# Ada rows on GpSimd's queue, and in the first stage in three small places of their own

## The chip, the cores and the metric

The kernel runs on one NeuronCore of a Trainium2 chip. The metric is the device time of one execution in microseconds. The engines are called as in the profile: PE (TensorE, with PEld for its weight loads), DVE (VectorE), ACT (ScalarE), POOL (GpSimd) and SP (SyncE). SP and POOL issue transfers; each engine takes its instructions in order.

## What is computed

One transformer layer for 256 tokens of width 2048, in float32. Nine vectors that depend on a condition `c` shift, scale and gate its three parts:

```python
ada = (silu(c) @ w_ada + b_ada)              # [9 * 2048]; w_ada is 2048 x 18432
sh1, sc1, g1, sh2, sc2, g2, sh3, sc3, g3 = split(ada, 9)
h = swiglu(modulate(x, sh1, sc1), ffn1_w_in, ffn1_w_out)          # 2048 -> 2 x 5632 -> 2048
x = layernorm(ALPHA * x + 0.5 * (1 + g1) * h, ln1_g, ln1_b)
h = token_mixer(modulate(x, sh2, sc2), ...)                       # FoX attention and mLSTM heads
x = layernorm(ALPHA * x + (1 + g2) * h, ln2_g, ln2_b)
h = swiglu(modulate(x, sh3, sc3), ffn2_w_in, ffn2_w_out)
x = layernorm(ALPHA * x + 0.5 * (1 + g3) * h, ln3_g, ln3_b)
# modulate(x, sh, sc) = layernorm(x) * (1 + sc) + sh
```

## The kernel before

**Products.** Each weight is brought in as float32 into a large place (tag `raw`, three places of 1 MB) by SP in `load_w` (L371). `split` makes two float32r parts of it: ACT casts the high part (L145) and DVE subtracts it for the low part (L146). The parts lie in six places each, two to a block of 1 MB. `mm3` then takes three matmuls (L388 to L390) for one product.

**Ada rows.** `w_ada` is not multiplied on PE. One row block holds 128 rows by 1024 columns (512 KB); 16 of them make an item. DVE multiplies the first by a column of silu(c) (L158) and adds each further one with a multiply-add (L160) into an accumulator; PE then sums over the partitions by products with ones. `ada_acc` is the helper, and its instructions stay in program order. The small places (tag `araw`, three places of 512 KB) hold such rows; a layernorm's scratch `sq` takes one of them for a while.

**The first stage.** The first matrix of the first feed-forward part is taken in four rounds `j`, each over 512 of the 2048 inputs and twelve blocks of 1 MB in an order given by `order_of(j)`. `first_in` makes the 48 matmuls of a block; the part sums of rounds after the first are added by DVE (L809). A round can begin when its 512 columns of x are modulated, which needs the shift and scale columns, and so 16 ada rows. The rows of round 0 come before all else. Those of round j + 1 are taken during round j by the generator `first_ada`, which is advanced once in most blocks: each call issues two rows and adds them. Two calls of three put the two rows into one large place (L715), the third into two small ones (L709). After the last, PE sums the columns (L736, L752 for round 0), DVE writes `scsh`, and `modulate_both` makes the columns of x. `behind(modulated[0])` queues the adds on DVE behind the last part of the modulation before.

**Later stages.** 14 more items follow, for the gates (`ada_gate`) and the other shifts and scales (`ada_pair`). `pump` is called once per block or so; it first adds the rows that were issued before (`add_landed`) and then issues a few more (`ada_rows`, L168), on SP's queue, into the small places. `need(n)` completes n items where their result is used. The bias of a gate is a transfer on POOL's queue (L208), which waits until the gate's place in `gate` has been read for the last time. POOL also computes the powers for the layernorms (`inv_root`, L268) and the masks of the mixer.

The order of the instructions on each engine and each queue is made ahead of time by a planner from program order and its own costs. DVE's order is written out by hand at the layernorms (`boundary`) and DVE's and ACT's for the end of round 0's rows.

Of the kernel before, what the change touches and what calls it, by code (L numbers as in the profile page):

```python
# [7 lines left out]
F32 = mybir.dt.float32  # L8
F32R = mybir.dt.float32r
AF = mybir.ActivationFunctionType  # L10
ALU = mybir.AluOpType
# [3 lines left out]
P = 128  # L15
T = 256
D = 2048
KD = D // P
# [29 lines left out]
def layer_kernel(  # L48
# [8 lines left out]
    V, S, G_, PE, SP = nc.vector, nc.scalar, nc.gpsimd, nc.tensor, nc.sync  # L57
# [16 lines left out]
    ap = ctx.enter_context(tc.tile_pool(name="ap", bufs=1))  # L74
# [4 lines left out]
    def mm_tile(name):  # L79
        return pm.tile([P, 512], F32, tag="mm", name=name)  # L80

    def aux_tile(name):
        return pa.tile([P, 512], F32, tag="aux", name=name)
# [13 lines left out]
    ones, onesr = triu1[:, P:], trir[:, P:]  # L97
# [8 lines left out]
    cps = aux_tile("cps")  # L106
# [4 lines left out]
    bcol = cst.tile([P, 9, KD], F32, name="bcol")  # L111
# [17 lines left out]
    def load_mixer_smalls():  # L129
        hrow = ap.tile([6, 1024], F32, tag="acc", name="hrow")  # L130
        SP.dma_start(hrow[0:4, :], mlstm_conv_w[0])
        SP.dma_start(hrow[4:5, :], mlstm_conv_b)
        SP.dma_start(hrow[5:6, :], mlstm_norm_g)
        SP.dma_start(gbias[:, 0:8], fox_f_bias[0:1, :].to_broadcast([P, 8]))
        SP.dma_start(gbias[:, 8:12], mlstm_i_bias[0:1, :].to_broadcast([P, 4]))
        SP.dma_start(gbias[:, 12:16], mlstm_f_bias[0:1, :].to_broadcast([P, 4]))
        yield
        hps = aux_tile("hps")
        for i in range(8):
            PE.transpose(hps[:, i * 6:(i + 1) * 6], hrow[:, i * P:(i + 1) * P], ident[:6, :6])  # L140
        V.tensor_copy(hcol.rearrange("p a b -> p (a b)"), hps[:, :48])
# [7 lines left out]
    scsh = cst.tile([P, 9, KD], F32, name="scsh")  # L149
    gate = cst.tile([P, D], F32, name="gate")  # L150


    def pair_cols(v, j):
        return w_ada[0, :, v * D:(v + 2) * D].rearrange("k (v n) -> k v n", v=2)[:, :, j * 512:(j + 1) * 512]

    def ada_acc(acc, raw, k):
        if k == 0:
            ins = V.tensor_scalar_mul(acc, raw, csil[:, k:k + 1])  # L158
        else:
            ins = V.scalar_tensor_tensor(out=acc, in0=raw, scalar=csil[:, k:k + 1], in1=acc,  # L160
                                         op0=ALU.mult, op1=ALU.add)
        tc.keep_in_program_order(ins)


    def ada_rows(acc, src, tag):
        for k in range(KD):
            raw = ap.tile([P, 1024], F32, tag="araw", bufs=3, name=f"ar{tag}_{k}")
            SP.dma_start(raw.rearrange("p (v n) -> p v n", v=2), src[k * P:(k + 1) * P])  # L168
            landing.append((acc, raw, k))
            yield PAUSE if k == KD - 1 else None  # L170

# [121 lines left out]
    def ntag():  # L293
        seq[0] += 1
        return str(seq[0])
# [3 lines left out]
    modulated = [None]  # L299

    def behind(ins):
        return tc.issue_after(ins.ins) if ins else nullcontext()

    def modulate_both(v, j, rs, xT):
        xf = npool.tile([P, 4, T], F32, tag="xf", name=f"xf{ntag()}")
        n = xf.rearrange("p k t -> p (k t)").rearrange("p (a n) -> p a n", a=2)
        for a in range(2):
            S.activation(n[:, a, :], res[:, a, j * 512:(j + 1) * 512], AF.Identity, bias=rs[a][:, 1:2],
                         scale=rs[a][:, 0:1])
        yield  # L310
        tps = [aux_tile(f"tp{ntag()}") for _ in range(2)]
        for q in range(4):
            for a in range(2):
                PE.transpose(tps[q // 2][:, (2 * (q % 2) + a) * P:(2 * (q % 2) + a + 1) * P],
                             n[:, a, q * P:(q + 1) * P], ident)
        yield
        for q in range(4):
            k = 4 * j + q
            S.activation(xf[:, q, :], tps[q // 2][:, (q % 2) * T:(q % 2 + 1) * T], AF.Identity,
                         bias=scsh[:, v, k:k + 1], scale=scsh[:, v + 1, k:k + 1])  # L320
            hi, lo = (x[:, k, :] for x in xT)
            S.copy(hi, xf[:, q, :])
            yield
            modulated[0] = V.tensor_tensor(out=lo, in0=xf[:, q, :], in1=hi.bitcast(F32), op=ALU.subtract)
            yield
# [33 lines left out]
    def new_xT(tag):  # L359
        return (xp.tile([P, KD, T], F32R, name=f"xhi_{tag}"), xp.tile([P, KD, T], F32R, name=f"xlo_{tag}"))  # L360
# [332 lines left out]
    xT = new_xT("f1")  # L693
# [3 lines left out]
    def first_ada(j, ws=iter(())):  # L697
        src = pair_cols(0, j)
        if j % 2:
            acc = ap.tile([P, 2, 512], F32, tag="acc", name=f"acc0_{j}")  # L700
        else:
            acc = gate[:, :1024].rearrange("p (v n) -> p v n", v=2)
        for kk in range(8):
            if kk % 3 == 2:
                raws = []
                for h in range(2):
                    k = 2 * kk + h
                    raw = ap.tile([P, 2, 512], F32, tag="araw", bufs=3, name=f"ar0_{j}_{k}")
                    SP.dma_start(raw, src[k * P:(k + 1) * P])  # L709
                    raws.append(raw)  # L710
            else:
                raw = wp.tile([P, 2, 2, 512], F32, tag="raw", bufs=3, name=f"ar0_{j}_{kk}")
                for h in range(2):
                    k = 2 * kk + h
                    SP.dma_start(raw[:, h], src[k * P:(k + 1) * P])  # L715
                raws = [raw[:, h] for h in range(2)]
            with behind(modulated[0]):
                for h in range(2):
                    k = 2 * kk + h
                    if k < KD - 1:  # L720
                        ada_acc(acc, raws[h], k)
                    else:
                        for b in range(2):
                            bs = slice(b * 256, (b + 1) * 256)
                            ada_acc(acc[:, :, bs], raws[h][:, :, bs], k)
            if kk == 5:
                mb = modulate_both(0, j, rs0, xT)
            if kk in (5, 6):
                next(mb)
            yield  # L730
        cps = aux_tile(f"cp{j}"), mm_tile(f"cq{j}") if j == 0 else None

        def columns():
            for q in range(4):
                for v in range(2):
                    PE.matmul(cps[0][:, 4 * v + q:4 * v + q + 1], acc[:, v, q * P:(q + 1) * P], ones[:, 0:1],  # L736
                              start=True, stop=True)
            js = slice(4 * j, 4 * j + 4)
            V.tensor_tensor(out=scsh[:, 0:2, js], in0=cps[0][:, :8].rearrange("p (v k) -> p v k", v=2),
                            in1=bcol[:, 0:2, js], op=ALU.add)  # L740

        if j:
            columns()
            for _ in mb:
                pass
            yield
            return

        def column(q):
            cp = cps[q % 2][:, q:q + 2]  # L750
            for v in range(2):
                PE.matmul(cp[:, v:v + 1], acc[:, v, q * P:(q + 1) * P], ones[:, 0:1], start=True, stop=True)  # L752
            k = 4 * j + q
            V.tensor_tensor(out=scsh[:, 0:2, k:k + 1], in0=cp.unsqueeze(2), in1=bcol[:, 0:2, k:k + 1], op=ALU.add)

        column(0)
        next(mb)
        column(1)
        next(mb)
        next(mb)  # L760
        column(2)
        next(ws, None)
        next(mb)
        column(3)
        next(mb)
        next(ws, None)
        for _ in mb:
            pass
        yield


    NS = 12

# [60 lines left out]
    fa = first_ada(0, ws_halves())  # L834
    rs0 = [small(2, "mr", f"mr_x{a}") for a in range(2)]
# [16 lines left out]
                   ada_pair(6, 1), ada_gate(5, 0, 1.0), ada_gate(5, 1, 1.0), ada_pair(6, 2), ada_pair(6, 3),  # L852
                   ada_gate(8, 0, 0.5), ada_gate(8, 1, 0.5)]
    for j in range(4):
        fa = first_ada(j + 1) if j < 3 else load_mixer_smalls()
        for n, i in enumerate(order_of(j)):
            w = list(ws if n + j == 0 else first_w(j, i))
            for _ in range(n not in (4, 9, 10)):
                next(fa, 0)
            first_in(j, n, i, w)  # L860
            if j == 3 and n > 2:
                pump(R_F)
# [59 lines left out]
    xT = new_xT("mx")  # L922
    raws = [mo_raw(u) for u in range(3)]
    mow = {}
    fence, _, xs = boundary(*ent["f"], lgb, 3, "1", xT, entry_of(mo_load, mow, 3, 6), KD)
# [337 lines left out]
    for j in (2, 3, 0, 1):  # L1263
        ps = form_a_pair(C_FQ + j * 256, C_FK + j * 256, f"f{j}")
        for i in range(2):
            h = 2 * j + i
# [66 lines left out]
    xT = new_xT("f2")  # L1333
# [31 lines left out]
    for j in range(2, 10):  # L1365
# [3 lines left out]
        if j == 7:  # L1369
            need(11)  # L1370
            mb = modulate_both(6, 2, mr2, xT)
            next(mb)
        ps = half_in(j, 0, "fh")
        for f in range(2):
            i = 2 * j + f
# [11 lines left out]
    mb = []  # L1387
# [7 lines left out]
    for j in range(2, 10):  # L1395
# [7 lines left out]
        for f in range(2):  # L1403
            i = 2 * j + f
# [51 lines left out]
```

## Time and profile before

| | us |
|---|---|
| median of three runs (lowest, highest) | 1946.42 (1943.57, 1947.09) |
| the profiled execution: its time | 1946.44 |
| the profiled execution: span of its instructions | 1944.7 |
| PE busy | 1893.7 |
| DVE busy | 1458.4 |
| ACT busy | 931.4 |
| POOL busy | 19.4 |

The span is the time from the first to the last instruction. The page gives the busy time of each engine, its share of the span, and the number of instructions. Matmuls overlap one another, so PE counts as busy while any is under way; whether it runs at its usual pace is read from the starts of the matmuls. Queries of the trace give the same numbers for stretches of the span (windows), the waits of each engine with what ended them, the instructions in order of time, and the chain of waits that ended last. The columns of a row are told where one is shown. A row of a wait reads: engine, what it was about to do and its line, what it waited for; then the sum in microseconds, how often, and the longest.

### The profile page before, as it was taken

What the parts mean: (1) busy time and instruction counts of PE and PEld (TensorE: products, weight loads), DVE (VectorE), ACT (ScalarE), POOL (GpSimd) and SP (SyncE); (2) the same over time, 40 slices, a digit from 0 to 9 for tenths busy, and PEclk for the clock granted to TensorE, in tenths of its full rate; (3) what the DMA queues carried; (4) which work ended last, traced back from release to release, by engine and by line L of the source; (5) the groups of instructions that cost most, each with busy time, mean ns of one, the idle gap of its engine ahead of it and who ended that gap; (6) DMA issues with size and microseconds to landing.
All of it is one profiled execution on the core that took longest, in us unless ns stands there. A gap on an engine that the chain in (4) does not pass through costs nothing.

```text
span 1944.7 us, 32312 instructions
## 1 busy us (share of the span) xinstructions
PE 1893.7 (97%) x13197; PEld 1737.9 (89%) x13197; DVE 1458.4 (75%) x1753; ACT 931.4 (48%) x1294; POOL 19.4 (1%) x37
## 2 busy tenths in 40 slices
PE   3999999999999999999999999999999999999997
PEld 3999999999988888699999886999999999988886
DVE  7879879777678898678787787677776554555776
ACT  2544354444354454745664644565444444444552
POOL 0000000000000000000000000000000000000000
PEclk9999999999999999999999999999999999999999
DMA  8999969999898798489878884997787755655552
GB/s 324 349 321 318 316 206 313 319 305 332 287 324 306 260 312 270 152 295 305 272 245 281 292 287 148 310 322 266 238 269 253 236 185 192 233 192 195 194 191 90
DMA packets 301963, 510.89 MB, mean 263 GB/s; under 512 B 10834, under 2 KB 158962, under 8 KB 300792
## 3 DMA queue, kind: packets, MB, share of 16 engines
q1 hardware_dynamic: 300952, 505.70, 76.9%
q0 software_dynamic: 864, 3.15, 0.5%
q8 instruction: 103, 1.69, 0.4%
q14 instruction: 44, 0.36, 0.0%
HBM read 506.71 MB, written 2.10 MB: 262 GB/s over the span
## 4 chain that ended last, share of the span: by engine, by line
PE 72%; issue 11%; DVE 9%; DMA 5%; ACT 2%; POOL 0%; SPq 0%; DVEq 0%; ACTq 0%; POOLq 0%
PE gu_f L389 8%; PE gu_f L388 8%; PE gu_f L390 8%; PE o_f L388 8%; PE o_f L390 8%; PE o_f L389 8%; PE s L388 3%; PE s L390 3%; PE s L389 2%; DMA raw_s<-in_ffn_w_in_dram 2%; DMA raw_mxo<-in_w_out_dram 2%; DVE gate L160 2%; PE fh L388 2%; PE fh L389 1%; PE fh L390 1%
## 5 line engine op out<-in xcount | busy, mean ns | idle before, releaser
L160 DVE SCALAR_TENSOR_TENSOR acc<-ar,csil,acc 128x1024 f32<-128x1024 f32 x242 | 307.2, 1270 | 23.2 <-DMA ar<-in_w_ada_dram 22.3
L388 PE MATMUL s<-xhi_f,hi_s 128*128 128x256 f32 x768 | 214.1, 279 | 1.8 <-ACT hi_s L145 1.8
L390 PE MATMUL s<-xhi_f,lo_s 128*128 128x256 f32 x768 | 213.5, 279 | 1.1 <-DVE lo_s L146 1.1
L389 PE MATMUL s<-xlo_f,hi_s 128*128 128x256 f32 x768 | 213.5, 278 | 0.0
L390 PE MATMUL gu_f<-xhi_f,lo_f2i 128*128 128x256 f32 x768 | 212.0, 276 | 0.0
L389 PE MATMUL gu_f<-xlo_f,hi_f2i 128*128 128x256 f32 x768 | 212.0, 276 | 0.0
L388 PE MATMUL gu_f<-xhi_f,hi_f2i 128*128 128x256 f32 x768 | 212.0, 276 | 0.0
L146 DVE TENSOR_TENSOR lo_f2i<-raw_f2i,hi_f2i 128x1024 fp32r<-128x1024 f32 x96 | 117.6, 1225 | 99.8 <-ACT hi_f2i L145 99.7
L388 PE MATMUL gu_f<-xhi_f,hi_f1i 128*128 128x256 f32 x640 | 176.8, 276 | 0.0
L390 PE MATMUL gu_f<-xhi_f,lo_f1i 128*128 128x256 f32 x640 | 176.7, 276 | 0.0
L389 PE MATMUL gu_f<-xlo_f,hi_f1i 128*128 128x256 f32 x640 | 176.7, 276 | 0.0
L145 ACT CAST hi_f2i<-raw_f2i 128x1024 fp32r<-128x1024 f32 x96 | 100.8, 1050 | 137.5 <-PE gu_f L389 125.5
L145 ACT CAST hi_s<-raw_s 128x1024 fp32r<-128x1024 f32 x96 | 97.3, 1048 | 114.4 <-DMA raw_s<-in_ffn_w_in_dram 70.1
L388 PEld LDWEIGHTS s<-xhi_f,hi_s 128*128 128x128 f32 x768 | 145.6, 190 | 2.3 <-ACT hi_s L145 2.3
L390 PEld LDWEIGHTS s<-xhi_f,lo_s 128*128 128x128 f32 x768 | 145.4, 190 | 2.0 <-DVE lo_s L146 2.0
L389 PEld LDWEIGHTS s<-xlo_f,hi_s 128*128 128x128 f32 x768 | 145.7, 190 | 0.0
L389 PEld LDWEIGHTS gu_f<-xlo_f,hi_f2i 128*128 128x128 f32 x768 | 144.2, 188 | 0.1
L388 PEld LDWEIGHTS gu_f<-xhi_f,hi_f2i 128*128 128x128 f32 x768 | 144.2, 188 | 0.1
L390 PEld LDWEIGHTS gu_f<-xhi_f,lo_f2i 128*128 128x128 f32 x768 | 144.2, 188 | 0.0
L146 DVE TENSOR_TENSOR lo_s<-raw_s,hi_s 128x1024 fp32r<-128x1024 f32 x96 | 114.4, 1220 | 38.0 <-ACT hi_s L145 37.7
L145 ACT CAST hh<-hT 128x512 fp32r<-128x512 f32 x128 | 78.6, 621 | 132.7 <-PE o_f L389 132.5
L146 DVE TENSOR_TENSOR lo_f2o<-raw_f2o,hi_f2o 128x1024 fp32r<-128x1024 f32 x88 | 107.7, 1224 | 44.9 <-ACT hi_f2o L145 44.8
(480 smaller groups left out, 5340.7 us busy)
## 6 DMA issues: line engine op xcount, KB each, us to landing
ar<-in_w_ada_dram SPq DMA_DIRECT2D x288, 512.0 KB, 5.9
raw_s<-in_ffn_w_in_dram SPq DMA_DIRECT2D x48, 1024.0 KB, 5.6
raw_f2i<-in_ffn_w_in_dram SPq DMA_DIRECT2D x48, 1024.0 KB, 5.2
raw_f1o<-in_ffn_w_out_dram SPq DMA_DIRECT2D x44, 1024.0 KB, 7.2
raw_f2o<-in_ffn_w_out_dram SPq DMA_DIRECT2D x44, 1024.0 KB, 5.1
raw_f1i<-in_ffn_w_in_dram SPq DMA_DIRECT2D x40, 1024.0 KB, 7.6
raw_mxo<-in_w_out_dram SPq DMA_DIRECT2D x16, 1024.0 KB, 8.6
raw_fh<-in_ffn_w_in_dram SPq DMA_DIRECT2D x16, 1024.0 KB, 7.9
```

Of the source, the lines that this page charges most:

```text
L145: S.copy(hi, src)
L146: V.tensor_tensor(out=lo, in0=src, in1=hi.bitcast(F32), op=ALU.subtract)
L160: ins = V.scalar_tensor_tensor(out=acc, in0=raw, scalar=csil[:, k:k + 1], in1=acc, op0=ALU.mult, op1=ALU.add)
L388: PE.matmul(o, ah, bh, start=start, stop=False)
L389: PE.matmul(o, ah, bl, start=False, stop=False)
L390: return PE.matmul(o, al, bh, start=False, stop=stop)
```

## The change

Ada rows of the later stages are issued from POOL's queue instead of SP's (`ada_rows`). In the first stage, `first_ada` keeps only the rows of round 0, on SP's queue and in large and small places as before. The rows of the other rounds come from a new generator, `next_ada`: it issues two rows per call from POOL's queue, all into the three small places, and adds the two rows of the call before. It has one call more than `first_ada` had, and the loop gives it one more block.

```diff
@@ ada_rows
-            SP.dma_start(raw.rearrange("p (v n) -> p v n", v=2), src[k * P:(k + 1) * P])
+            G_.dma_start(raw.rearrange("p (v n) -> p v n", v=2), src[k * P:(k + 1) * P])
@@ first_ada: its part for j > 0 goes
-        cps = aux_tile(f"cp{j}"), mm_tile(f"cq{j}") if j == 0 else None
-
-        def columns():
-            ...
-        if j:
-            columns()
-            for _ in mb:
-                pass
-            yield
-            return
+        cps = aux_tile(f"cp{j}"), mm_tile(f"cq{j}")
@@ new
+    def next_ada(j):
+        src = pair_cols(0, j)
+        if j % 2:
+            acc = ap.tile([P, 2, 512], F32, tag="acc", name=f"acc0_{j}")
+        else:
+            acc = gate[:, :1024].rearrange("p (v n) -> p v n", v=2)
+        rows = []
+        for k in range(0, KD + 2, 2):
+            with behind(modulated[0]):
+                for raw in rows:
+                    ada_acc(acc, raw, k - 2 + rows.index(raw))
+            rows = []
+            for h in range(2 if k < KD else 0):
+                raw = ap.tile([P, 2, 512], F32, tag="araw", bufs=3, name=f"ar0_{j}_{k + h}")
+                G_.dma_start(raw, src[(k + h) * P:(k + h + 1) * P])
+                rows.append(raw)
+            if k == 10:
+                mb = modulate_both(0, j, rs0, xT)
+            if k in (10, 12):
+                next(mb)
+            yield
+        cp = aux_tile(f"cp{j}")
+        for i in range(8):
+            PE.matmul(cp[:, i:i + 1], acc[:, i // 4, i % 4 * P:(i % 4 + 1) * P], ones[:, 0:1], start=True, stop=True)
+        js = slice(4 * j, 4 * j + 4)
+        V.tensor_tensor(out=scsh[:, 0:2, js], in0=cp[:, :8].rearrange("p (v k) -> p v k", v=2),
+                        in1=bcol[:, 0:2, js], op=ALU.add)
+        for _ in mb:
+            pass
+        yield
@@ the loop over rounds
-        fa = first_ada(j + 1) if j < 3 else load_mixer_smalls()
+        fa = next_ada(j + 1) if j < 3 else load_mixer_smalls()
         for n, i in enumerate(order_of(j)):
             w = list(ws if n + j == 0 else first_w(j, i))
-            for _ in range(n not in (4, 9, 10)):
+            for _ in range(n not in (4, 9)):
                 next(fa, 0)
```

More of the change, by code (lines that the diff above doesn't have):

```diff
@@ L730, in first_ada @@
             yield
-        cps = aux_tile(f"cp{j}"), mm_tile(f"cq{j}") if j == 0 else None
-        def columns():
[L734 to L740, printed above, removed]
-        if j:
-            columns()
-            for _ in mb:
-                pass
-            yield
-            return
+        cps = aux_tile(f"cp{j}"), mm_tile(f"cq{j}")
         def column(q):
```

## The prediction

> **What bounds the kernel now.** I read the page's table of engines first, then the waits of TensorE, then the busy time by windows, then the matmuls in order of time.
>
> ```profile
> span 1944.7 us, 32312 instructions
> ...
> PE 1893.7 (97%) x13197; PEld 1737.9 (89%) x13197; DVE 1458.4 (75%) x1753; ACT 931.4 (48%) x1294; POOL 19.4 (1%) x37
> ...
> PE cp L752 <- DVE gate L160: 14.8, 1, 14.8
> ...
> 200.00:220.00 20.00, 20.00 (x179) 20.00 (x178) 18.49 (x21) 8.00 (x8) 0.00 (x0) 1.00 0.94 322
> 220.00:240.00 20.00, 18.06 (x143) 17.66 (x142) 17.40 (x21) 7.99 (x8) 0.00 (x0) 0.91 0.92 310
> ```
>
> TensorE (PE) is busy for 97% of the span. Its 51 us of idle time lie mostly in the first 38 us, where no weight product can start, and at the three layernorms. A change to transfers can therefore win only what TensorE loses to late data. The windows (columns: stretch, length, then PE, PEld, DVE, ACT and POOL busy with counts, the granted clock, DMA share, GB/s) show one clear loss: 143 matmuls where the window before has 179, with the granted clock at 0.91 instead of 1.00.
>
> ```profile
> 60.07 0.28 PE L389 MATMUL s<-xlo_f,hi_s 128*128 128x256 f32 x1
> ...
> 63.93 0.28 PE L390 MATMUL s<-xhi_f,lo_s 128*128 128x256 f32 x1
> ...
> 227.93 0.28 PE L390 MATMUL s<-xhi_f,lo_s 128*128 128x256 f32 x1
> 229.38 0.38 PE L388 MATMUL s<-xhi_f,hi_s 128*128 128x256 f32 x1 [1.18 <-ACT hi_s L145]
> 230.64 0.58 PE L390 MATMUL s<-xhi_f,lo_s 128*128 128x256 f32 x1 [0.76 <-DVE lo_s L146]
> 231.03 0.41 PE L388 MATMUL s<-xhi_f,hi_s 128*128 128x256 f32 x1
> ...
> 234.01 0.28 PE L390 MATMUL s<-xhi_f,lo_s 128*128 128x256 f32 x1
> ```
>
> From 60.07 to 63.93 there are 34 steps, so a matmul of the first stage takes 3.86 / 34 = 0.1135 us, and a block of 48 takes 5.45 us. From 227.93 to 234.01 there are 18 steps, which should take 2.04 us and take 6.08: **4.04 us are lost**. TensorE waits 1.18 and 0.76 us for split weights, and then runs at a step of 0.21 us until 233.80. The rest of what late data cost shows between the column sums of the blocks of x (16 matmuls each, in order of time):
>
> ```profile
> 102.25 1.84 PE L736 MATMUL cp<-trir,acc 128*128 128x1 f32 x16
> 170.92 1.84 PE L736 MATMUL cp<-trir,gate 128*128 128x1 f32 x16
> 242.97 1.84 PE L736 MATMUL cp<-trir,acc 128*128 128x1 f32 x16
> ```
>
> A round needs 576 x 0.1135 = 65.4 us, 1.7 for the column sums and about 0.8 for eight transposes: 67.9. The first interval is 68.67, the second 72.05. The losses are 0.8 and 4.15, together 4.9 us, of which the hole is 4.04.
>
> Why were the weights late? The chain of waits at that place, then SyncE's own waits and those of the engines from 38 to 245 us (us, times, longest):
>
> ```profile
> 220.62 1.21 DVE acc L160
> 221.85 6.34 DMA raw_s<-in_ffn_w_in_dram
> 228.29 1.05 ACT hi_s L145
> ...
> SPq L371 <- DVE lo_s L146: 68.8, 29, 6.2
> SPq L715 <- DVE lo_s L146: 18.6, 7, 3.5
> SPq L371 <- DVE acc L160: 11.7, 6, 3.7
> ...
> ACT hi_s L145 <- DMA raw_s<-in_ffn_w_in_dram: 70.1, 27, 7.4
> ```
>
> A pair of ada rows held one of the three large `raw` places until its add ended at 221.83; only then could SyncE issue the weights, which took 6.34 us to land. SyncE issues in order, so a row that waits for a place (L715) also holds back the weights behind it.
>
> **The change part by part.** The first edit moves 224 rows (14 items of 16, L168) from SyncE's queue to POOL's, the second 48 of the first stage (three rounds of 16, L709 and L715). Only the 16 rows of the first round stay. The nearest row for a transfer issued by POOL is the bias of the gates, of equal size (512 KB):
>
> ```profile
> L208 POOL DMA_DIRECT2D gate<-in_b_ada_dram x6: 527/599/732, 173.1 to 1196.5; - x6
> DMA to landing us min/median/max: 4.1/5.2/7.3
> ```
>
> 272 issues of 0.6 us are 163 us on POOL, idle 99% of the span: hidden, if nothing urgent stands behind them. SyncE loses as many issues; what they covered was its own queue.
>
> *The large places* then belong to weights. Three blocks (16 us) can be on their way where rows took a share, and the delay from the add at 221.83 to the split goes. I credit the hole, 4.0, and 0.8 of the other 0.9: **-4.8 us**. Bounds: 0 (nothing cured) and -4.9. Late next would be VectorE's own throughput, so here is its load in the three rounds:
>
> ```profile
> 38.50:104.20 65.70, 65.62 (x554) 64.93 (x555) 51.37 (x48) 39.67 (x53) 0.00 (x0) 1.00 0.93 330
> 104.20:174.50 70.30, 69.98 (x616) 69.78 (x616) 60.76 (x68) 30.85 (x38) 0.73 (x1) 1.00 0.94 325
> 174.50:245.30 70.80, 68.86 (x591) 68.46 (x590) 62.73 (x70) 29.22 (x35) 0.00 (x0) 0.98 0.91 312
> ```
>
> VectorE is busy 51.4 + 60.8 + 62.7 = 174.9 of 206.8 us. It can follow TensorE, with 31.9 us to spare. Its work stays the same; the last row of a round is added undivided, which moves it by less than 0.2 us.
>
> *Three small places, two rows per block.* A row's place is free when its add ends; the row three further on must have landed one block later. VectorE's work in such a block is two splits, two adds and, after the first round, two part sums:
>
> ```profile
> L146 DVE TENSOR_TENSOR lo_s<-raw_s,hi_s x75: 1214/1219/1227, 38.5 to 242.8; 128x1024 fp32r<-128x1024 f32 x75
> L160 DVE SCALAR_TENSOR_TENSOR acc<-ar,csil,acc x16: 746/1278/1286, 179.5 to 224.9; 128x1024 f32<-128x1024 f32 x14, 128x512 f32<-128x512 f32 x2
> L809 DVE TENSOR_TENSOR hT<-hT,s x62: 675/680/689, 120.7 to 317.7; 128x512 f32<-128x512 f32 x62
> ```
>
> That is 2 x 1.22 + 2 x 1.28 = 5.0 us in the first round and 5.0 + 2 x 0.68 = 6.4 after it. Issue and landing at the median are 5.2 us (the row of landings above), with up to 0.6 more because a row goes in two pieces per partition. At 5.8 the pairs of the first round wait 0.8 us each, 8 x 0.8 = 6 us inside that round's 14 us of spare time (65.7 - 51.4), and the later ones nothing. I take **0**; the bounds stand with the rivals. "Added a block behind" only shifts the adds; column sums still stand before the twelfth block.
>
> *The start.* The first rows of the second round now leave POOL as soon as a small place is free, beside the last rows and the first weights of the first round:
>
> ```profile
> 20.22 4.87 SPq L715 DMA_DIRECT2D ar<-in_w_ada_dram  x4
> ...
> 26.85 0.37 SPq L371 DMA_DIRECT2D raw_s<-in_ffn_w_in_dram  x1
> ...
> DMA to landing us min/median/max: 3.9/6.8/11.6
> ...
> 33.46 0.77 DVE gate L160
> ...
> 20.00:40.00 20.00, 4.96 (x21) 4.62 (x22) 16.90 (x23) 4.27 (x8) 0.00 (x0) 1.00 0.97 350
> ```
>
> A row is 0.52 MB / 350 GB/s = 1.5 us of the DMA engines. The last row was issued at about 24.7 us (the last of the four), rows up to 50 us land after 6.8 at the median, so at 31.5, and VectorE uses it at 33.46. Two microseconds are to spare: one extra row is covered, a second costs 1.0 at most, and as much may hit the first weights (issued at 26.85). Cost between 0 and 1.5; I take **+0.3**, near the covered end, since the second and third place come free only with the adds of rows ten and eleven.
>
> *The moved queue.* Behind a row on POOL now stand the powers of the layernorms (L268), the memsets of the mixer, and the gate biases (L208); VectorE waits for the powers. At a layernorm:
>
> ```profile
> 768.53 27.07 SPq L168 DMA_DIRECT2D ar<-in_w_ada_dram  x3
> ...
> 796.14 0.55 POOL L268 TENSOR_TENSOR mr<-sums,mhalf 128x1 f32<-128x1 f32 x1 [7.61 <-DVE sums L558]
> 797.65 0.93 PE L340 MATMUL tp<-ident,n 128*128 128x128 f32 x4 [0.54 <-ACT n L336]
> ...
> 676.37 0.53 POOL L208 DMA_DIRECT2D gate<-in_b_ada_dram  x1 [404.70 <-DVE o_f L466]
> ...
> 1012.77 1.65 POOL L268 TENSOR_TENSOR rr<-ss,mhalf 128x8 f32<-128x8 f32 x1 [183.73 <-DVE ss L1202]
> ```
>
> SyncE's third row there waits for the square's scratch (`sq`, a small place), free about when the power at 796.14 runs. If POOL issues that row first, the power comes 0.53 to 0.73 us later, and TensorE, already waiting 0.54 us, with it. Three such places (two layernorms, the mixer at 1012.77) give 0 to 2.2; I take **+0.3**. A gate bias waits for the gate's last reader (404.7 us while POOL had nothing else); it was queued when it became ready, so rows behind it would wait only for the planner's error: 0. SyncE no longer waits at L168 in later stages, but TensorE shows no waits for weights there: 0.
>
> Sum, against the profiled execution (1946.44, its span 1944.7 and 1.74 around it; the median of the runs is 1946.42): 1946.4 - 4.8 + 0.3 + 0.3 = **1942.2 us**, 0.22% less. About 0.2% (3.9 us) is what a measurement of this kernel can tell from no change, so the forecast lies at that edge.
>
> **The rivals.** *The small ring starves VectorE (slower).* Weighted over 24 pairs VectorE's own work between them is (8 x 5.0 + 16 x 6.4) / 24 = 5.9 us, and the spare time 31.9 / 24 = 1.3, so it decides from 7.2 us of issue and landing. The bias row's maximum is 7.3 and with a longer issue 7.9; then VectorE lacks 24 x 0.7 = 17 us, and the time is 1942.2 + 17 = 1959; half-way, 1951. For it speaks a DMA share of 0.91 to 0.94 in these rounds, against it the median of 5.2. A POOL that could not issue while VectorE runs an add would get there from 5.8 + 1.28 = 7.1: at the deciding point, 1942 to 1944.
> The Trainium skill, in "SBUF — State Buffer", § SBUF: two separate sides, warns that POOL cannot write descriptors while VectorE holds the shared port in a 2-port mode. Were the adds and splits such operations, the sum by it would be the 1944 above; the bias issues, made while VectorE was busy, kept to 0.73 us, so this trace shows no such lock.
>
> *Nothing is gained (same).* The bytes and the engines that move them are the same, and the rounds already run at 0.91 to 0.94. If weights land later by what the rows take beside them, the hole stays: 1946.4. Against it: the hole began with a place held by an add, not with a full set of DMA engines.
> The Trainium skill says so in "DMA: Bandwidth & Descriptors", § Issuing engines are not separate DMA queues: all queues interleave on the same 16 engines, and a second issuer saves only issue time. By it the sum would be 1946; the trace shows SyncE's in-order waits (68.8 + 18.6 + 11.7 us) besides.
>
> *Cured, but given back.* With the start at its bound of 1.5 and POOL's delays at 2.2, 1946.4 - 4.8 + 3.7 = 1945.3.
>
> **How the numbers follow.** The hole closes and little is given back: 0.55, own range 1940.5 to 1944, of which 0.42 below 1942.5 and 0.13 above. Nothing gained: 0.13; given back: 0.12. Starved: 0.20. Faster 0.42, same 0.38, slower 0.20. The range goes from 1940 (all of 4.9 cured and 1.5 more in places I can't see) to 1952, the half-way price of starving; some 0.1 lies above it and 0.1 below.
>
> **What would show it.** In the window from 220 to 240 us some 179 matmuls and a clock of 1.00; ScalarE's waits for `raw_s` well below 70.1 us; the second and third column sums 68 us apart. Waits of VectorE's adds for `ar` of over 30 us before 245 us would show the starving; landings above 7.2 us are its cause. A later first weight product than 38.5 us shows the start's cost; powers behind rows on POOL with longer waits of TensorE at the layernorms show the queue's. The prediction is wrong if a new hole opens elsewhere, since a wait of 1.2 us cost 4 here.

## The result: 1952.8 us, slower by 0.36%

The changed kernel takes 1952.79 us (median of 7; 1951.18 to 1953.31), the kernel before beside it 1945.38 (median of 7; 1942.55 to 1948.73): a ratio of 1.0036, 95% interval 1.0025 to 1.0047. The span of the profiled execution went from 1944.7 to 1951.0 us. The forecast was 1942.2, and the time lies just above its range.

The first stage did what was forecast. Rows of the changed kernel: the window of the former hole, the column sums (L779 is now their line; 16 matmuls each, first and last start at the end), the first weight product, and ScalarE's waits for raw weights (us, times, longest):

```profile
220.00:240.00 20.00, 20.00 (x179) 20.00 (x179) 18.15 (x21) 8.41 (x8) 1.65 (x3) 1.00 0.94 331
...
L779 PE MATMUL cp<-trir,acc x16: 164/250/250, 101.9 to 103.5; 128*128 128x1 f32 x16
L779 PE MATMUL cp<-trir,gate x16: 166/250/250, 169.9 to 171.5; 128*128 128x1 f32 x16
L779 PE MATMUL cp<-trir,acc x16: 164/250/250, 237.9 to 239.5; 128*128 128x1 f32 x16
...
39.02 0.58 PE L388 MATMUL s<-xhi_f,hi_s 128*128 128x256 f32 x1 [1.04 <-ACT hi_s L145]
...
ACT hi_s L145 <- DMA raw_s<-in_ffn_w_in_dram: 18.6, 8, 5.6
```

There are 179 matmuls in the window at a full clock (143 before). The column sums follow 68.0 us apart, twice, as the prediction's sum of 67.9 says. ScalarE waits 18.6 us where it waited 70.1.

The gain was lost later. POOL's powers at the layernorms are good milestones, since each is followed by the same work: first the power at the first layernorm (`rs`), then the one in the mixer (`rr`), then the second layernorm's (`rs`); the kernel before, then the changed one.

```profile
776.35 1.53 POOL L268 TENSOR_TENSOR rs<-mv,mhalf 128x1 f32<-128x1 f32 x1 [99.45 <-DVE mv L280]
...
1186.38 1.53 POOL L268 TENSOR_TENSOR rs<-mv,mhalf 128x1 f32<-128x1 f32 x1 [25.50 <-DVE mv L280]
```
```profile
771.38 1.52 POOL L268 TENSOR_TENSOR rs<-mv,mhalf 128x1 f32<-128x1 f32 x1 [25.00 <-DVE mv L280]
...
1008.22 1.68 POOL L268 TENSOR_TENSOR rr<-ss,mhalf 128x8 f32<-128x8 f32 x1 [0.65 <-DVE ss L1217]
...
1192.16 1.53 POOL L268 TENSOR_TENSOR rs<-mv,mhalf 128x1 f32<-128x1 f32 x1 [22.06 <-DVE mv L280]
```

With `rr` of the kernel before at 1012.77 (shown above), the changed kernel is 4.97 us ahead at the first, 4.55 ahead at the second and 5.78 behind at the third. So 10.3 us went inside the mixer: its stretch from `rr` to `rs` takes 183.94 us, 173.61 before. The windows by stage and TensorE's waits of the changed kernel say the same:

```profile
38.00:245.00 207.00, 205.94 (x1799) 205.65 (x1800) 176.16 (x185) 106.36 (x135) 34.78 (x49) 1.00 0.92 325
...
1008.00:1192.00 184.00, 174.89 (x984) 152.41 (x983) 138.11 (x187) 84.13 (x147) 22.03 (x33) 0.97 0.76 262
```
```profile
PE ytp L1235 <- DVE gate L214: 4.6, 1, 4.6
PE yps L1094 <- DVE gate L214: 4.0, 1, 4.0
```

TensorE waits twice for L214, the last step of a gate (DVE adds the summed rows, read from PSUM, to the bias). That step frees the PSUM place that the next work of TensorE needs: transposes of y (`ytp`) at the first of the two places, products (`yps`) at the second. Here is the first place: VectorE, POOL and TensorE of the changed kernel, each in order of time.

```profile
1017.65 1.28 DVE L160 SCALAR_TENSOR_TENSOR acc<-ar,csil,acc 128x1024 f32<-128x1024 f32 x1
...
1022.09 1.23 DVE L146 TENSOR_TENSOR lo_f1a<-raw_f1a,hi_f1a 128x1024 fp32r<-128x1024 f32 x1 [0.88 <-ACT hi_f1a L145]
1026.79 1.28 DVE L160 SCALAR_TENSOR_TENSOR acc<-ar,csil,acc 128x1024 f32<-128x1024 f32 x1 [3.47 <-DMA ar<-in_w_ada_dram]
1027.99 1.28 DVE L214 SCALAR_TENSOR_TENSOR gate<-bc,gate 128x512 f32<-128x512 f32 x2
...
1019.24 0.59 POOL L168 DMA_DIRECT2D ar<-in_w_ada_dram  x1 [9.34 <-DVE acc L160]
1023.32 1.05 POOL L168 DMA_DIRECT2D ar<-in_w_ada_dram  x2 [3.50 <-PE bc L180]
...
1028.73 0.66 PE L1235 MATMUL ytp<-ident,og 128*128 128x128 f32 x4 [4.55 <-DVE gate L214]
1029.73 0.42 PE L389 MATMUL pr_f<-xlo_mx,hi_f0b 128*128 128x256 f32 x1
...
1032.50 0.41 PE L390 MATMUL pr_f<-xhi_mx,lo_f0b 128*128 128x256 f32 x1
```

VectorE at the same place in the kernel before:

```profile
1026.57 1.22 DVE L146 TENSOR_TENSOR lo_f1a<-raw_f1a,hi_f1a 128x1024 fp32r<-128x1024 f32 x1 [0.85 <-ACT hi_f1a L145]
1027.71 1.28 DVE L214 SCALAR_TENSOR_TENSOR gate<-bc,gate 128x512 f32<-128x512 f32 x2
...
1031.40 1.29 DVE L160 SCALAR_TENSOR_TENSOR acc<-ar,csil,acc 128x1024 f32<-128x1024 f32 x1 [0.88 <-DMA ar<-in_w_ada_dram]
```

The reader is to see an exchange of two instructions. Before, the gate step comes straight behind the split, and the add of the next row later. With the change the add stands ahead of the gate step. Its row could not be there: a gate's sum (`ada_sum`) holds two of the three small places until PE's products with ones (L180) have read them, so a row has the third place only, and is issued when the add before it ends (1018.9). It is added 8 us after that, in both kernels (1023.4 to 1031.4 before). VectorE waits 3.47 us for it, the gate step with it, and TensorE 4.55 us with the gate step. Afterwards TensorE steps at (1032.50 - 1029.73) / 13 = 0.213 us in place of 0.118.

The Trainium skill, "TensorE: Matmul & The Clock Gate", § What's actually happening, says that about 3.4 us without work halve the clock, and that it takes about 3.4 us of work to come back. The trace agrees at this place: 4.55 us of waiting, then some 3.2 us of slow steps. It does not agree at the hole of the kernel before, where waits of 1.18 and 0.76 us were followed by slow steps until 233.80, nor at the second place below, with 5.7 us of them behind 4.01.

At the second place two adds wait ahead of the gate step. VectorE and TensorE of the changed kernel, then VectorE of the kernel before:

```profile
1105.57 1.28 DVE L160 SCALAR_TENSOR_TENSOR acc<-ar,csil,acc 128x1024 f32<-128x1024 f32 x1 [3.71 <-DMA ar<-in_w_ada_dram]
...
1112.70 1.29 DVE L160 SCALAR_TENSOR_TENSOR acc<-ar,csil,acc 128x1024 f32<-128x1024 f32 x1 [3.57 <-DMA ar<-in_w_ada_dram]
...
1115.04 1.28 DVE L214 SCALAR_TENSOR_TENSOR gate<-bc,gate 128x512 f32<-128x512 f32 x2
...
1115.77 1.22 PE L1094 MATMUL yps<-pT,yF 128*128 128x256 f32 x2 [4.01 <-DVE gate L214]
...
1120.21 0.63 PE L389 MATMUL o_mx<-lo_mxo,yh 128*128 128x512 f32 x1
```
```profile
1100.78 1.27 DVE L160 SCALAR_TENSOR_TENSOR acc<-ar,csil,acc 128x1024 f32<-128x1024 f32 x1
...
1105.99 1.28 DVE L160 SCALAR_TENSOR_TENSOR acc<-ar,csil,acc 128x1024 f32<-128x1024 f32 x1 [0.60 <-DMA ar<-in_w_ada_dram]
1109.68 1.29 DVE L214 SCALAR_TENSOR_TENSOR gate<-bc,gate 128x512 f32<-128x512 f32 x2 [2.42 <-PE bc L180]
```

Here no add was moved past the gate step: the kernel before has the same two adds ahead of it. What differs is when their rows are there. Before, they were issued at 1093.89 and 1102.07 and added 6.9 and 3.9 us later; with the change they were issued at 1096.10 and 1107.15 and added 9.5 and 5.5 us later. VectorE, which before was early and waited 2.42 us for PE's sums, now comes late.

A matmul that takes 0.39 us at full pace takes 0.63 here, with steps of 0.43 for 0.23, until 1121.5. The two waits are 8.6 us, the slow steps behind them some 1.6 and 2.6 (17 x 0.095, and 5.7 us at a little over half pace), 12.8 us together. That is more than the 10.3 us above; the next section has a kernel against which the mixer loses 12.4.

### The profile page after: what moved, and what is told of

Its sections match the earlier page's. It is cut to its first block, busy times and chain, and to the rows that moved or that the text cites. A ratio compares the mean times of both kernels' runs of the same rounds, so it can differ in the third digit from the quotient of the medians.

```text
span 1951.0 us, 32388 instructions
## 1 busy us (share of the span) xinstructions
PE 1894.4 (97%) x13197; PEld 1738.7 (89%) x13197; DVE 1456.1 (75%) x1750; ACT 933.8 (48%) x1294; POOL 198.1 (10%) x309
## 4 chain that ended last, share of the span: by engine, by line
PE 86%; DVE 6%; DMA 4%; issue 2%; ACT 2%; POOL 0%; DVEq 0%; SPq 0%; ACTq 0%; POOLq 0%
PE gu_f L390 8%; PE gu_f L388 8%; PE gu_f L389 8%; PE o_f L388 8%; PE o_f L390 8%; PE o_f L389 8%; PE s L388 5%; PE s L390 5%; PE s L389 4%; DMA ar<-in_w_ada_dram 2%; PE fh L388 1%; PE fh L389 1%; PE fh L390 1%; PE fs L390 1%; PE fs L389 1%
## 5 line engine op out<-in xcount | busy, mean ns | idle before, releaser
L168 POOL DMA_DIRECT2D ar<-in_w_ada_dram x224 | 143.9, 643 | 1023.6 <-DVE acc L160 736.6
```

Source lines behind the costliest of these rows:

```text
L168: G_.dma_start(raw.rearrange("p (v n) -> p v n", v=2), src[k * P:(k + 1) * P])
```

## The experiments

Theory A: the loss comes only from moving the rows of L168 off SyncE's queue, because VectorE's order then has adds of rows ahead of work that TensorE waits for. Rival B: POOL and its queue (listed in the profile as `software_dynamic`, those of SyncE and ScalarE as `hardware_dynamic`) cost something wherever they are used. Rival C: the first stage's edit displaces everything behind it, and the order follows from that. Four kernels (the first stage alone, the later rows alone, the new places, one order mended) ran on one chip against the kernel before at 1943.91 us, the four others on a second against 1944.63; the two repeats of the new places ran on a third.

**The first stage alone.** Changed kernel, with

```diff
@@ ada_rows
-            G_.dma_start(raw.rearrange("p (v n) -> p v n", v=2), src[k * P:(k + 1) * P])
+            SP.dma_start(raw.rearrange("p (v n) -> p v n", v=2), src[k * P:(k + 1) * P])
```

> The change in the first stage alone: the 48 rows of the x blocks go through POOL and the small places, the 224 rows of L168 stay on SyncE's queue. Theory A (the loss of 10.3 us in the mixer comes only from moving the rows of L168: the add of a row is ordered ahead of the gate's sum L214, and the row is not there): the first stage's gain stays and nothing is lost later, 1945.4 - 4.8 = 1940.6 us, ratio 0.997 to 0.998; TensorE's wait for the gate before the transposes of y stays at 0.6 us or less. Rival B (POOL and its queue cost something wherever they are used: longer landings, a second queue beside the weights): some of the gain is missing, 1943 to 1946. Rival C (the first stage's edit shifts everything behind it by some 5 us and the mixer meets another order by that): the loss stays, about 1951.

Measured: 1939.9 us (1938.16 to 1940.93), ratio 0.9976 (0.9966 to 0.9987). The gate step is back in its place ahead of the add:

```profile
1023.53 1.28 DVE L214 SCALAR_TENSOR_TENSOR gate<-bc,gate 128x512 f32<-128x512 f32 x2
...
1026.95 1.28 DVE L160 SCALAR_TENSOR_TENSOR acc<-ar,csil,acc 128x1024 f32<-128x1024 f32 x1 [0.60 <-DMA ar<-in_w_ada_dram]
...
1008.00:1192.00 184.00, 183.12 (x1048) 158.64 (x1047) 149.11 (x212) 89.58 (x161) 5.41 (x7) 1.00 0.77 267
```

The mixer's stretch takes 171.5 us, 12.4 less than with the whole change, from which this kernel differs in that one line. Rival C falls: the same displacement of the first stage is here, and no loss.

**The later rows alone.** The kernel before, with the opposite line at L168.

> Only the rows of L168 moved to POOL's queue, the first stage as before. Theory A: the mixer loses its 10.3 us without the 4.8 of gain, 1954 to 1957 us, ratio 1.0045 to 1.006, with waits of TensorE of 4 us or more for the gate's sum L214 before the transposes of y at two places. Rival B: the same sign, but spread over the stages, with no single wait over 2 us. Rival C: no loss, 1944 to 1947.

Measured: 1958.33 us (1957.22 to 1960.56), ratio 1.0072 (1.006 to 1.0084), a little above what A gave. TensorE's waits:

```profile
PE yps L1079 <- DVE gate L214: 4.7, 1, 4.7
PE ytp L1220 <- DVE gate L214: 4.4, 1, 4.4
```

The mixer's stretch takes 184.7 us, 11.1 more than before; the profiled execution (span 1955.3) is 10.6 us over that of the kernel before, so between these two executions nearly all is lost there. The medians are 14.4 us apart; no trace shows where the other 4 us lie.

**New places, old queue.** Changed kernel with SP in place of POOL at L168 and L770.

> The new first stage (three small places, two rows per block of weights, added a block behind), but all rows on SyncE's queue as before. If the places alone cured the hole at 227.93 us (my prediction's term of -4.8): as the first-stage-only kernel, 1940 to 1942 us, and ScalarE's wait for raw weights falls as it did with the change (from 70.1 to 18.6 us). If the queue was needed for it (a row that waits for its small place holds up the weights behind it on SyncE): 1943 to 1950, with ScalarE's wait for raw weights above 40 us.

Measured: 1943.36 us (11 runs, 1941.05 to 1947.77), ratio 0.9996 (0.9987 to 1.0006); ScalarE waits 54.1 us (38.7 and 60.3 in the two repeats below). The profiled execution was one of its fastest, so the same kernel ran twice more:

> The kernel with the new places and all rows on SyncE's queue once more: its executions lie between 1941 and 1948 us, those of the first-stage-only kernel between 1938 and 1941. If SyncE's queue in the first stage makes the difference, a slower execution than the first profiled one (1941.4) shows lost matmuls between 38 and 245 us (fewer than 1783 there) and nothing elsewhere. If the difference lies in the later stages, the first stage has again some 1783 to 1790 matmuls and the loss is behind 245 us.

> The same kernel a third time, for the same question: where an execution that is slower than 1941.4 us loses its time. With SyncE's queue as the cause, between 38 and 245 us, by one or two holes of 1 to 4 us; otherwise behind 245 us.

They took 1944.52 and 1944.68 us. The first stage of the three, in the order 1941.41, 1944.52 and 1944.68, then the windows of the first:

```profile
38.00:245.00 207.00, 205.38 (x1783) 204.43 (x1784) 175.08 (x184) 103.28 (x134) 0.73 (x1) 1.00 0.92 321
```
```profile
38.00:245.00 207.00, 203.06 (x1758) 201.59 (x1759) 173.18 (x181) 100.75 (x127) 0.73 (x1) 1.00 0.92 320
```
```profile
38.00:245.00 207.00, 203.84 (x1752) 202.10 (x1752) 172.31 (x179) 100.38 (x126) 0.73 (x1) 1.00 0.91 316
```
```profile
60.00:80.00 20.00, 18.96 (x165) 18.56 (x164) 15.15 (x13) 11.07 (x14) 0.00 (x0) 1.00 0.92 330
220.00:240.00 20.00, 20.00 (x180) 20.00 (x178) 19.31 (x22) 7.45 (x8) 0.00 (x0) 1.00 0.96 334
```

The hole at 228 us is gone in all three. But matmuls are lost elsewhere in the stage (14 between 60 and 80 us in the first), and the slower executions lose some 25 to 30 more, most of them between 60 and 120 us; the mixer's stretch is 171.4 to 172.0 us in all. In the slower two the first layernorm's power comes at 775.94 and 776.76 us, where the kernel before has 776.35: the new places alone gained nothing there. This kernel differs from the first stage alone only in the queue of the first stage's rows. SyncE's waits from 38 to 245 us, with the rows on its own queue and then (first stage alone) on POOL's:

```profile
SPq L371 <- DVE lo_s L146: 44.8, 20, 3.5
SPq L770 <- DVE acc L160: 42.4, 26, 5.3
```
```profile
SPq L371 <- DVE lo_s L146: 164.2, 37, 7.5
```

A row that waits for a small place (L770) holds back the weights behind it; without rows SyncE waits for nothing but the weights' own places. Both parts of the edit are needed for the whole gain.

**The queue alone in the first stage.** The kernel before, with POOL for rounds 1 to 3 at L709 and L715, in the large and small places as before:

```diff
-                    SP.dma_start(raw, src[k * P:(k + 1) * P])
+                    (G_ if j else SP).dma_start(raw, src[k * P:(k + 1) * P])
...
-                    SP.dma_start(raw[:, h], src[k * P:(k + 1) * P])
+                    (G_ if j else SP).dma_start(raw[:, h], src[k * P:(k + 1) * P])
```

> The kernel before with the queue alone changed in the first stage: the 48 rows of the second to fourth round on POOL, but in the places of before (two pairs of three in a large place of the weights); the rows of L168 on SyncE. If the large places made the hole at 227.93 us (my prediction's -4.8 is for them): as before, 1942 to 1946 us, ScalarE's wait for raw weights above 60 us. If the rows in SyncE's queue made it: 1938 to 1941, ScalarE's wait near 25 us.

Measured: 1956.21 us (1954.17 to 1957.71), ratio 1.0057 (1.0043 to 1.0071). Neither time was expected, though ScalarE's wait is above 60 us as the first said:

```profile
38.00:245.00 207.00, 195.27 (x1643) 192.86 (x1643) 161.93 (x168) 92.71 (x119) 31.64 (x44) 0.98 0.87 300
...
ACT hi_s L145 <- DMA raw_s<-in_ffn_w_in_dram: 94.2, 31, 8.4
```

With the rows on another queue the large places became worse: 156 matmuls fewer than with the whole change, and ScalarE waits 94.2 us for weights. The first layernorm's power comes 13.2 us later than before and the mixer's stretch is 171.5 us, so the loss is all ahead of that layernorm. The window from 220 to 240 us has 174 matmuls, so the hole there is nearly gone in this way too, and larger ones are elsewhere. That rows and weights take turns at three places by an order that no longer matches the queues is my reading; it was not taken apart further.

**One order mended.** The changed kernel, with the add of an item's third row queued on VectorE behind the last gate step before it:

```diff
@@ ada_gate
-                V.scalar_tensor_tensor(out=g, in0=next(bcs), ...)
+                gate_sum[0] = V.scalar_tensor_tensor(out=g, in0=next(bcs), ...)
@@ add_landed
-            ada_acc(*landing.pop(0))
+            row = landing.pop(0)
+            with behind(gate_sum[0] if row[2] == 2 else None):
+                ada_acc(*row)
+            if row[2] == 2:
+                gate_sum[0] = None
```

> The changed kernel with one order added: the add of an item's third row comes behind the gate's sum L214 of the item before. All rows stay on POOL. Theory A: the 4.6 and 4.0 us waits of TensorE go, with the slow steps behind them, some 10 us come back: 1941 to 1943 us, ratio to the kernel before 0.9975 to 0.9985. Rival B (POOL's longer landing is the loss, whatever the order): the adds' waits for rows (54.7 us) and the time stay, above 1949. In between, 1944 to 1948, if TensorE's wait for the gate goes but another takes its place.

Measured: 1945.46 us (1942.72 to 1948.5), ratio 1.0005 (0.9996 to 1.0015): the case in between. The wait for the gate is gone and another is there (TensorE's waits, then VectorE's from 1090 to 1130 us):

```profile
PE ptp L1089 <- ACT s L1084: 4.0, 3, 2.0
...
PE ytp L1240 <- DVE gate L214: 0.2, 1, 0.2
```
```profile
DVE acc L160 <- DMA ar<-in_w_ada_dram: 9.8, 5, 4.0
```

With all rows still on POOL the mixer's stretch falls from 183.9 to 177.8 us, so 6 us hang on whether these adds stand ahead of the gate step. At the first place the edit restores the order of before; at the second it makes one that the kernel before did not have. The rest, 4 us against the kernel before, is my reading: five adds wait 9.8 us for rows, VectorE comes late to the scores of a head (`s`, L1079), and TensorE waits 4.0 us for their transposes.

**ScalarE's queue for the later rows.** The changed kernel with `S.dma_start` at L168, a hardware queue with no weights in it. VectorE's order at the first place has the add ahead there too.

> The changed kernel with the 224 rows of L168 on ScalarE's queue in place of POOL's: a hardware queue like SyncE's, that has no weights in it. VectorE's order has the add of the third row ahead of the gate's sum L214 at (5,0), as with POOL. Theory A (the order is what costs: an add that was put early since its row no longer stands behind the weights of SyncE's queue): the gate's wait before the transposes of y stays at 3 to 5 us and the time stays high, 1947 to 1953 us. Rival B (the software queue of POOL is slow to land): it goes, 1939 to 1942.

Measured: 1949.78 us (1947.26 to 1953.65), ratio 1.0027 (1.0015 to 1.0039); the mixer's stretch takes 184.0 us, as with POOL.

```profile
PE ytp L1235 <- DVE gate L214: 3.4, 1, 3.4
PE ptp L1084 <- ACT s L1079: 2.8, 1, 2.8
```

So it isn't POOL's queue as such. The landings in the mixer as a whole say the same: from issue to landing (min, median, max, L168 from 1008 to 1192 us) on SyncE's queue before, on POOL's with the change, on ScalarE's here:

```profile
DMA to landing us min/median/max: 3.8/5.6/10.3
```
```profile
DMA to landing us min/median/max: 4.2/5.9/9.4
```
```profile
DMA to landing us min/median/max: 4.2/6.3/10.9
```

Rival B falls with that, and with the two converse kernels that follow. The medians hide the second place, though. In the five kernels with the mixer's rows on SyncE, the first of the two adds there comes 6.9 to 7.1 us after its row's issue and waits for nothing. In the five others it waits for its row, and comes 8.4 us (ScalarE) or 9.5 to 12.1 us (POOL) after the issue. So this row lands later off SyncE's queue, whichever other queue it is on. Why it does is open: on SyncE's queue it stands ahead of the weights issued behind it, but no run tried that.

**The mixer's items back on SyncE, and the converse.** Five items, (6,0), (6,1), (5,0), (5,1) and (6,2), have their rows at or in the mixer: 80 of 224.

```diff
@@ ada_rows
-            G_.dma_start(raw.rearrange("p (v n) -> p v n", v=2), src[k * P:(k + 1) * P])
+            (SP if tag in ("6_0", "6_1", "5_0", "5_1", "6_2") else G_).dma_start(
+                raw.rearrange("p (v n) -> p v n", v=2), src[k * P:(k + 1) * P])
```

> The changed kernel with only the 80 rows of five items ((6,0), (6,1), (5,0), (5,1), (6,2): those that are added in or at the mixer) back on SyncE's queue; the other 144 rows of L168 and the 48 of the first stage stay on POOL. VectorE's order at both gate sums is that of the first-stage-only kernel. Theory A: the whole loss is gone, 1938 to 1942 us, and rows on POOL cost nothing in the FFN stages. Rival B: 144 of 224 rows still pay, some 7 of the 11 us of loss stay, 1946 to 1949.

Measured: 1940.32 us (1939.14 to 1941.94), ratio 0.9977 (0.9968 to 0.9985), the mixer's stretch 171.4 us. The converse has SP and `G_` exchanged:

> The converse of the kernel with the mixer's items on SyncE: of the 224 rows of L168 only the 80 of the five items in the mixer go on POOL, the other 144 on SyncE; the first stage as changed. Theory A: the whole loss is there, 1949 to 1953 us, with the two waits of TensorE for L214 of 4 us or more. Rival B: 80 of 224 rows pay their share, some 4 of 11 us, 1943 to 1945.

Measured: 1952.32 us (1951.73 to 1953.94), ratio 1.004 (1.0027 to 1.0053), the stretch 185.0 us, with

```profile
PE ytp L1235 <- DVE gate L214: 4.4, 1, 4.4
PE yps L1094 <- DVE gate L214: 4.1, 1, 4.1
```

144 rows on POOL cost nothing outside the mixer; 80 in it cost the whole loss. Of all kernels tried, those with the whole change in the first stage and the mixer's rows on SyncE are the fastest: 1939.9 and 1940.3 us, 0.24% and 0.23% less than before.

The runs show where the loss is: with the mixer's rows off SyncE's queue it is there, with them on it it is not. An add that was put ahead of the gate step is shown at the first place only; at the second, rows were late for the order of before. What stays open: the planner makes VectorE's order from costs of its own. That it takes a row off SyncE's queue to be there sooner is a reading of its orders at the first place. With the mixer's rows on POOL (three kernels) or ScalarE (one) the add stands ahead of the gate step, in a fifth it was held back by hand, and in the five kernels with these rows on SyncE it stands behind. Why it does so was not tried. Also open is some 2 us of the mixer's stretch: 173.6 in the kernel before, 171.4 to 172.0 in each other kernel with SyncE's rows there, without a wait that explains it.

## Why the prediction was wrong

*The large places* (-4.8, bounds 0 to -4.9): right in kind, and a little short. From the first weight product to the third column sums the changed kernel takes 237.9 - 39.02 = 198.9 us, the kernel before 242.97 - 38.50 = 204.5: -5.6, of which 4.05 in the round of the hole. But I credited the places alone. With the rows still on SyncE's queue the median gains nothing that can be told (0.9996), and with the queue alone the kernel loses 11.6 us. The hole at 228 us went with the places, but on SyncE's queue others opened ahead of it; the stage as a whole needed both. That the term came out is in part luck: the change had both parts. The hole's size is of one execution, too: with the later rows alone moved, and the first stage as before, the same window has 161 matmuls and not 143.

*Three small places* (0): right in the sum. VectorE's adds wait 9.7 and 2.6 us for rows in the three rounds, inside the spare time, though rows landed after 6.7 us at the median and not 5.2. The starving rival needed over 30 us there.

*The start* (+0.3): the first weight product came at 39.02, 0.5 us later than before.

*The moved queue* (+0.3): this is the step that failed. Its powers stayed within their bounds of 0 to 2.2: from the first power to the last at a layernorm 19.95 us for 19.79 at the first and 20.21 for 19.80 at the second, together 0.6. The failure is in its last sentences. "A gate bias [...] only for the planner's error: 0" and "SyncE no longer waits at L168 in later stages, but TensorE shows no waits for weights there: 0" both ask what the queues gain or lose. They don't ask what VectorE does with rows that the planner now takes to be early (the first place), or that land later (the second). In place of 0 the mixer lost 10.3 us, 12.4 against the kernel that keeps the later rows on SyncE. Two facts in front of me would have led there: that the planner orders VectorE by its own costs, and that a gate's sum takes two of the three small places, so that its next rows come one at a time, 7 to 8 us each.

*The rivals.* Starving had the right mechanism, an add that waits for a row in the small ring, at the wrong place: the first stage has 31.9 us to spare, while in the mixer the ring is down to one place just when TensorE needs VectorE. "Nothing is gained" fell: the Trainium skill's rule behind it ("DMA: Bandwidth & Descriptors", § Issuing engines are not separate DMA queues) says that the queues interleave on the same engines; over the mixer the landings were indeed near one another on three queues (medians 5.6, 5.9 and 6.3 us), but the row at the second place came at most 7.1 us after its issue on SyncE's queue, and 8.4 to 12.1 on the others. And the queue moved the time both ways, through what stands behind what: on SyncE a waiting row delays weights, and off it an add is put early or its row lands late.

*What would show it* named a new hole elsewhere, and that "a wait of 1.2 us cost 4". Waits of 4.55 and 4.01 cost some 6 each. That the time lies only 0.8 us above the range is luck: the upper end, 1952, was the half-way price of a starving that did not occur.

## What to carry to other kernels

Where a planner fixes the order of each engine, a transfer moved to a freer queue can change the order of the engine that uses its data, and the moment at which the data is there. Compare that engine's order before and after, and ask of each use that moved up, or now waits, what stands behind it and who waits for that. Count the places that are free at that moment, not those that exist: two of three were held by the gate's sum. Move transfers stage by stage; here one stage earned 5 us, two cost nothing, and one lost 10.

## What the runs showed of the hardware

Over the mixer the queue that issues a 512 KB row hardly changes its landing: medians of 5.6 (SyncE), 5.9 (POOL) and 6.3 us (ScalarE). For one row at the second place it did: at most 7.1 us from issue to add on SyncE's queue, 8.4 on ScalarE's and 9.5 to 12.1 on POOL's. The slow steps behind a wait weren't in proportion to it: 3.2 us behind 4.55, 5.7 us behind 4.01. Rows on SyncE in the first stage also spread the times, 1941.1 to 1947.8 us over 11 runs; with them on POOL it was 1938.2 to 1940.9 over 7, and 1939.1 to 1941.9 over 11 with the 144 rows outside the mixer there too. The kernel with one order mended, also with them on POOL, spread from 1942.7 to 1948.5 us, so a spread has other causes as well.
